# Five late modulation vectors: from TensorE products between the up products to VectorE multiplies and ScalarE row sums

## The chip, the cores and the metric

The kernel runs on one core of one Trainium2 chip, as one program in one launch. The metric is the device time of an execution in microseconds. Three runs of the kernel before gave 2391.55 (the median), 2391.75 and 2386.89 us.

## The reference, cut to what matters

Two trunk layers act on 1152 tokens of 1024 channels: 1024 sample tokens (stream 0, conditioned by `c`) and 128 prompt tokens (stream 1, conditioned by `c_ctx`). What is conditioned comes from six modulation vectors per layer and stream:

```
def modulation(cond, w_mod, b_mod):
    m = jax.nn.silu(cond) @ w_mod + b_mod          # (1024) @ (1024, 6144)
    return jnp.split(m[:, None, :], N_MOD, axis=-1)

def run_layer(x, cond, mixer, w_mod, b_mod, g_mix_pre, g_mix_post, g_ff_pre, g_ff_post, w_ff1, w_ff2):
    sh1, sc1, gt1, sh2, sc2, gt2 = modulation(cond, w_mod, b_mod)
    h = rmsnorm(x, g_mix_pre) * (1.0 + sc1) + sh1
    y, aux = mixer(h)
    x = x + gt1 * rmsnorm(y, g_mix_post)
    h = rmsnorm(x, g_ff_pre) * (1.0 + sc2) + sh2
    x = x + gt2 * rmsnorm(sq_relu_mlp(h, w_ff1, w_ff2), g_ff_post)
    return x, aux
```

`sq_relu_mlp` is relu(h @ w1) squared, times w2, with 4096 hidden channels. Everything is fp32.

## The kernel before, in words

`build` (L261) runs, one after the other: `layer0_scan` (first norm, state-space scan, Fourier mixer), `glu`, and then for each layer `mixer_out` (projection out of the mixer and the norm that precedes the MLP), `ff_up` (up product, relu, square) and `ff_down`, with `layer1_mixer` between the layers. The order of the instructions on each engine is not the program's: a scheduler sets it when the program is built, from its own timing of the instructions. Every DMA is issued by SP, in one queue.

A matmul in full precision is made of three (`mm3`, L96): each operand is split into a high part (rounded by a ScalarE copy) and a low part (a VectorE subtraction), and high times high, high times low and low times high are added up in PSUM.

`ff_up` (L951) makes the hidden channels in 16 pairs of 128-channel blocks. `pair(p)` (L963) loads two weight tiles of 512 KB (`st`, L967), forms the seven weight sums of a Strassen-like scheme, splits them (L984, L985), and runs seven products, numbered 1, 2, 6, 5, 7, 3, 4, into three PSUM tiles `puA`, `puB`, `puC`. ScalarE copies sums out (`c`, L1036), VectorE takes differences (`h`, L1040), relu and square follow (L1042 on VectorE, L1064 and L1065 on ScalarE for the last one), VectorE forms four more sums (`hsum`, L1086), and eleven DMAs store the results (L1019, L1022). The last product of a pair ends in the row `h<-puA` at L1064: from one to the next is one pair. PSUM has one buffer for each of the three tiles, and the names rotate from pair to pair.

Ten pieces of modulation (of layer 0 `gt2`, of layer 1 `gt1`, `sc2`, `sh2`, `gt2`, each in two halves of 512 outputs) are the list `K.late` (L486); `ff_up` of layer 0 calls one of them after each of its pairs 0 to 9 (L1096). A job (`mod_chunk`, L110) loads four tiles of 512 KB of `w_mod`, two into slot `E` and two into the ring `wst`, runs matmuls `pmod` (L127) with the silu of the conditioning (`csil`, 2 columns in use of 32) as the stationary operand, copies the row out (`mrow`, L131), turns it by four transposes (`pmc`, L141), and VectorE adds the four partial sums, bias and gain (L143 to L146). A gate then takes another transpose (`pmg`, L157) and a store to DRAM (L159), from where `norm_load` reads it as a broadcast.

The ring `wst` has four buffers of 128 x 1160 fp32 (L294). In `ff_up` it holds the weight tiles `st`, the sum `u7` and the modulation tiles `mst`.

Of the kernel before, what the change touches and what calls it, by code (L numbers as in the profile page):

```python
# [17 lines left out]
D = 1024  # L18
# [21 lines left out]
class Slots:  # L40


    def __init__(self, K, *names):
        self.K, self.names, self.n = K, names, 0
# [6 lines left out]
def slot(K, n, shape, dtype=F32, name=None):  # L51

    return K.slab.tile(shape, dtype, name=name or n, tag=n)
# [207 lines left out]
def build(tc, A):  # L261
# [6 lines left out]
    with ExitStack() as top:  # L268
# [37 lines left out]
        mix = glu(K, gd, yd)  # L306
        for layer in range(2):
            xq = mixer_out(K, layer, mix)
            hd, hp = ff_up(K, layer, xq, K.late if layer == 0 else ())
            acts = ff_down(K, layer, hd, hp)  # L310
            if layer == 0:
                mix = layer1_mixer(K, acts)


def layer0_scan(K):
# [3 lines left out]
    with ExitStack() as ph:  # L319
# [160 lines left out]
        with tc.tile_pool(name="s5", bufs=1, side="right", reuse_waits="tile") as s5:  # L480
            dft = fnet_jobs(K, fp, zbs, yd)
            mods = mod_jobs(K, ((0, "gt1", 2, "g_mix_post"), (0, "sc2", 4, "g_ff_pre"), (0, "sh2", 3, None),
                                (1, "sc1", 1, "g_mix_pre"), (1, "sh1", 0, None), (0, "gt2", 5, "g_ff_post"), (1, "gt1", 2, "g_mix_post"),
                                (1, "sc2", 4, "g_ff_pre"), (1, "sh2", 3, None), (1, "gt2", 5, "g_ff_post")))
            jobs = [(dft if x == "f" else mods).pop(0) for x in JSEQ]
            K.late = dft + mods  # L486
            order = [s5, s5t, s5t]

            def inputs(hb):
                W = s5_inputs_of(K, s5, hb, zd[hb // 2])  # L490
                if hb not in efs:
                    pool = order[(hb + 1) % 3]
                    if hb in spill:
                        efs[hb] = pool.tile([128, 2176], F32, name="ef", tag="ef", bufs=2 if pool is s5t else 1)
                        nc.sync.dma_start(efs[hb], spill[hb])
                    else:
                        tables(hb, pool, True)
                W.m = s5_toeplitz(K, s5, hb)
                W.et, W.f = ef_views(efs[hb])
                return W  # L500

            W = inputs(0)
            held = None
            for hb in range(HB):
                s = s5_scan(K, s5, hb, W, fin)
                now = (hb, W, s, gd[hb // 2])
                if hb + 1 < HB:
                    W = inputs(hb + 1)
                if held:
                    s5_out(K, s5, *held)  # L510
                held = now
                for job in jobs[len(jobs) * hb // HB:len(jobs) * (hb + 1) // HB]:
                    job()
            s5_out(K, s5, *held)
# [433 lines left out]
    return xq  # L948


def ff_up(K, layer, xq, jobs):  # L951

    tc, nc, A = K.tc, K.nc, K.A
    v = nc.vector
    hd = [tc.dram_tile([4, 128, 7, 512], F32, name=f"hd{layer}_{c}") for c in range(4)]
    hp = [tc.dram_tile([128, 8, 2, 2, 32], F32, name=f"hp{layer}_{c}") for c in range(4)]
    hp2, hs = Slots(K, "W3", "W4", "W5"), Slots(K, "R4", "R6")
    K.mod_row = lambda: hs.tile([128, 512], F32, "mrow")
    K.mod_tag = "t"
    K.mod_pools = [(Slots(K, "E"), "mst"), (K.wst, "st")]  # L960
    K.mod_gather = 2

    def pair(p):  # L963
        raw = []
# [128 lines left out]

    for p in range(16):
        pair(p)
        if p < len(jobs):  # L1096
            jobs[p]()
    K.mod_gather = 1
    return hd, hp


# [747 lines left out]
def host_layout(inp):  # L1849
    f = lambda n: np.asarray(inp[n])  # L1850
    a = {}
# [14 lines left out]
    for l in range(2):  # L1866
        w = f(f"l{l}_w_mod").reshape(4, 2, 128, 12, 512)
        a[f"w_mod{l}"] = np.ascontiguousarray(w.transpose(3, 2, 0, 1, 4)).reshape(12, 128, 4, 1024)
    a["x_sample"] = f("x_sample").reshape(1024, 1024)
    xp = f("x_prompt").reshape(16, 8, 1024)  # L1870
    a["xp_perm"] = np.ascontiguousarray(xp[:, ::-1].transpose(1, 0, 2)).reshape(128, 1024)
# [106 lines left out]
```

## Time and profile before

| | us |
|---|---|
| three runs, median (lowest to highest) | 2391.55 (2386.89 to 2391.75) |
| the profiled execution | 2391.31 |
| its span, first to last instruction | 2389.5 |
| PE busy (95% of the span) | 2260.6 |
| PEld (weight loads, beside PE) | 1972.7 |
| VectorE (DVE) busy (70%) | 1668.0 |
| ScalarE (ACT) busy (42%) | 994.3 |
| GpSimd (POOL) busy | 195.0 |
| mean DMA rate over the span | 151 GB/s |

Busy time is how long at least one instruction of the engine was running. An engine's instructions may overlap at their ends, so that sums of single durations come out somewhat above it. "PEclk" is the TensorE clock that was granted, as a share of full speed; "DMA" is the mean busy share of the 16 DMA engines.

### The profile page before, as it was taken

The numbers are of one execution on the slowest core, as the hardware profiler recorded it, in microseconds if no ns is written. First come the engines' busy times: TensorE is split into PE (matmuls) and PEld (weight loads), VectorE is DVE, ScalarE is ACT, GpSimd is POOL, SyncE is SP. The second block draws the span as 40 slices with busy tenths as digits, with TensorE's granted clock in tenths as the row PEclk, the third lists the DMA queues.
The fourth block names the chain that finished last, engine by engine and source line by source line (L and its number), as shares of the span: only waits on it lengthen the run. The fifth ranks groups of instructions, "written<-read, shape, count | busy, mean of one in ns | idle before, by whom it ended". The sixth has DMA issues, their size and how long they took to land.

```text
span 2389.5 us, 34799 instructions
## 1 busy us (share of the span) xinstructions
PE 2260.6 (95%) x13462; PEld 1972.7 (83%) x13462; DVE 1668.0 (70%) x2628; ACT 994.3 (42%) x1718; POOL 195.0 (8%) x213
## 2 busy tenths in 40 slices
PE   7997676999999999999999899998999999999997
PEld 4996544987788899988888699887999999888886
DVE  7888999836755555757776854857666557677778
ACT  4543333647432233443343452457333333533332
POOL 0116773200000000000000000000000000000000
PEclk9998888999999999999999899999999999999999
DMA  8375675422465563744343431122344346544433
GB/s 300 131 276 161 195 240 164 144 96 98 157 213 178 177 199 118 253 150 153 114 148 102 135 125 46 63 97 97 112 148 139 120 148 229 170 130 134 144 108 141
DMA packets 200454, 361.49 MB, mean 151 GB/s; under 512 B 50064, under 2 KB 95760, under 8 KB 198240
## 3 DMA queue, kind: packets, MB, share of 16 engines
q1 hardware_dynamic: 200288, 359.26, 45.7%
q8 instruction: 106, 1.74, 0.3%
q14 instruction: 60, 0.49, 0.1%
HBM read 256.69 MB, written 102.51 MB: 150 GB/s over the span
## 4 chain that ended last, share of the span: by engine, by line
PE 82%; DVE 11%; ACT 2%; DMA 2%; issue 1%; POOL 1%; SPq 0%; DVEq 0%; ACTq 0%
PE pz L1284 8%; PE pz L1286 8%; PE pz L1287 8%; PE puA L97 6%; PE puA L99 6%; PE puA L98 6%; PE puC L97 3%; PE puC L99 3%; PE puC L98 3%; PE po L256 3%; PE po L258 3%; PE po L257 3%; DVE tp L1780 3%; PE pmod L127 2%; PE puB L98 1%
## 5 line engine op out<-in xcount | busy, mean ns | idle before, releaser
L1284 PE MATMUL pz<-wh,hh 128*128 128x512 f32 x840 | 326.0, 389 | 1.2 <-DVE z L1298 1.2
L1287 PE MATMUL pz<-wh,hl 128*128 128x512 f32 x840 | 326.8, 389 | 0.0
L1286 PE MATMUL pz<-wl,hh 128*128 128x512 f32 x840 | 326.8, 389 | 0.0
L1272 ACT ACTIVATE hh<-hr 128x1024 fp32r<-128x1024 f32 x96 | 96.9, 1009 | 262.9 <-PE pz L1286 231.7
L1284 PEld LDWEIGHTS pz<-wh,hh 128*128 128x128 f32 x840 | 157.7, 188 | 34.5 <-issue 2.0
L1287 PEld LDWEIGHTS pz<-wh,hl 128*128 128x128 f32 x840 | 157.7, 188 | 32.7
L1286 PEld LDWEIGHTS pz<-wl,hh 128*128 128x128 f32 x840 | 157.7, 188 | 32.5
L1273 DVE TENSOR_TENSOR hl<-hr,hh 128x1024 fp32r<-128x1024 f32 x96 | 110.9, 1156 | 91.7 <-ACT hh L1272 91.7
L1298 DVE TENSOR_TENSOR z<-z,pz 128x512 f32<-128x512 f32 x192 | 122.8, 682 | 31.6 <-PE pz L1287 31.1
L984 ACT ACTIVATE wh<-c 128x512 fp32r<-128x512 f32 x96 | 60.8, 633 | 175.7 <-DVE c L993 125.8
L1040 DVE TENSOR_TENSOR h<-puA,c 128x576 f32<-128x576 f32 (+1 forms) x34 | 24.6, 722 | 147.7 <-PE puA L99 147.7
L256 PE MATMUL po<-wh,act 128*128 128x512 f32 x288 | 112.5, 394 | 1.2 <-DVE rms L906 1.2
L257 PE MATMUL po<-wl,act 128*128 128x512 f32 x288 | 113.1, 393 | 0.0
L258 PE MATMUL po<-wh,act 128*128 128x512 f32 x288 | 113.0, 393 | 0.0
L984 ACT ACTIVATE wh<-st 128x512 fp32r<-128x512 f32 x96 | 57.3, 629 | 80.5 <-DMA st<-in_w_ff_dram 27.7
L1248 DVE TENSOR_TENSOR wl<-raw,wh 128x1024 fp32r<-128x1024 f32 (+1 forms) x64 | 73.2, 1154 | 24.0 <-ACT wh L1247 24.0
L985 DVE TENSOR_TENSOR wl<-c,wh 128x512 fp32r<-128x512 f32 x96 | 66.1, 688 | 32.1 <-ACT wh L984 31.6
L92 DVE TENSOR_TENSOR wl<-st,wh 128x1024 fp32r<-128x1024 f32 (+1 forms) x42 | 52.2, 1254 | 49.9 <-ACT wh L91 49.9
L1780 DVE TENSOR_TENSOR tp<-rt,xp 128x1168 f32<-128x1168 f32 x48 | 81.1, 1728 | 7.3 <-ACT xp L1773 6.8
L985 DVE TENSOR_TENSOR wl<-st,wh 128x512 fp32r<-128x512 f32 x96 | 63.6, 686 | 27.9 <-ACT wh L984 27.8
L1036 ACT ACTIVATE c<-puA 128x576 f32<-128x576 f32 (+1 forms) x68 | 42.2, 621 | 91.9 <-PE puA L99 88.5
L127 PE MATMUL pmod<-mst,csil 128*32 128x512 f32 x384 | 77.6, 675 | 1.2 <-DMA mst<-in_w_mod_dram 1.2
(505 smaller groups left out, 6725.3 us busy)
## 6 DMA issues: line engine op xcount, KB each, us to landing
hr<-hd SPq DMA_DIRECT2D x102, 512.0 KB
mst<-in_w_mod_dram SPq DMA_DIRECT2D x96, 512.0 KB
st<-in_w_ff_dram SPq DMA_DIRECT2D x68, 512.0 KB
hd<-hsum SPq DMA_DIRECT2D x120, 256.0 KB
raw<-in_w_ff_dram SPq DMA_DIRECT2D x56, 512.0 KB
hd<-h SPq DMA_DIRECT2D x98, 256.0 KB
ef<-ef SPq DMA_DIRECT2D x16, 1088.0 KB
xr<-xs SPq DMA_DIRECT2D x32, 512.0 KB
```

Source lines behind the costliest of these rows:

```text
L97: nc.tensor.matmul(ps, sh, mh, start=start, stop=False, skip_group_check=shared)
L98: nc.tensor.matmul(ps, sh, ml, start=False, stop=False, skip_group_check=shared)
L99: nc.tensor.matmul(ps, sl, mh, start=False, stop=stop, skip_group_check=shared)
L127: nc.tensor.matmul(ps[32 * j:32 * j + 32, :], K.csil[:, kb, :], st[:, 512 * k:512 * k + 512], start=kb < 4, stop=kb >= 4, skip_group_check ...
L256: K.nc.tensor.matmul(ps, ah[kb][:, c], wh[:, s], start=kb == 0, stop=False)
L257: K.nc.tensor.matmul(ps, ah[kb][:, c], wl[:, s], start=False, stop=False)
L258: K.nc.tensor.matmul(ps, al[kb][:, c], wh[:, s], start=False, stop=kb == 7)
L985: v.tensor_tensor(wl, x, wh.bitcast(F32), op=ALU.subtract)
L1284: nc.tensor.matmul(o, hh[:, q, t], wh[:, q], start=start and s == 0 and q == 0, stop=False, skip_group_check=True)
L1286: nc.tensor.matmul(o, hh[:, q, t], wl[:, q], start=False, stop=False, skip_group_check=True)
L1287: nc.tensor.matmul(o, hl[:, q, t], wh[:, q], start=False, stop=s == 1 and q == n - 1, skip_group_check=True)
L1780: v.tensor_tensor(t[:, k], R[:, k:k + 1].to_broadcast([128, 2, 4, SC]), x, op=ALU.mult)
```

## The change

The jobs of `K.late` are gone, and with them the matmuls, the four transposes and the row copies of these five vectors. In their place a class `LateMods` makes each vector as sums along rows. The host sends the five blocks of `w_mod` turned over (`w_modt`), so that a tile of 128 x 1024 has 128 outputs on partitions and the 1024 inputs along the row. The silu of the conditioning of one stream is held in slot `E` as a tile `cs` in which all partitions have the same row; it comes from DRAM (`csd`), to which two DMAs write it from `csil`, element by element. One unit is: a DMA of 512 KB, one VectorE multiply (128 x 1024, in place, L979), and one ScalarE copy with `accum_out` (L980), which gives one column of 128 outputs for one stream. Each tile is loaded and worked on twice, once for each stream. Layer 0 has four vectors, 2 x 4 x 8 = 64 units, spread over the 15 steps after pairs 1 to 15 (four or five a step); layer 1 has one vector, 16 units, one or two a step. A vector ends with bias and gain on VectorE, and a gate with one transpose (L999) and a store.

```diff
-            hd, hp = ff_up(K, layer, xq, K.late if layer == 0 else ())
+            hd, hp = ff_up(K, layer, xq)
...
-                                (1, "sc1", 1, "g_mix_pre"), (1, "sh1", 0, None), (0, "gt2", 5, "g_ff_post"), (1, "gt1", 2, "g_mix_post"),
-                                (1, "sc2", 4, "g_ff_pre"), (1, "sh2", 3, None), (1, "gt2", 5, "g_ff_post")))
+                                (1, "sc1", 1, "g_mix_pre"), (1, "sh1", 0, None)))
...
+LATE = (((0, "gt2", 5, "g_ff_post"), (1, "gt1", 2, "g_mix_post"), (1, "sc2", 4, "g_ff_pre"), (1, "sh2", 3, None)),
+        ((1, "gt2", 5, "g_ff_post"),))
+
+class LateMods:
+    def __init__(self, K, wanted):
...
+        self.units = [(s, n, b) for s in range(2) for n in range(len(wanted)) for b in range(8)]
+        self.total, self.stream = len(self.units), None
+
+    def step(self, k, steps):
+        K, nc = self.K, self.K.nc
+        while self.units and self.total - len(self.units) < self.total * (k + 1) // steps:
+            s, n, b = self.units.pop(0)
+            layer, _, piece, _ = self.wanted[n]
+            if s != self.stream:
+                self.stream = s
+                self.c = slot(K, "E", [128, D], F32, "cs")
+                row = K.csd[s]
+                nc.sync.dma_start(self.c, bass.AP(tensor=row.tensor, offset=row.offset, ap=[[0, 128], [1, D]]))
+            st = stage_tile(K, "mst")[:, :D]
+            nc.sync.dma_start(st, K.A["w_modt"][LATE_ROWS.index((layer, piece)), b])
+            nc.vector.tensor_tensor(st, st, self.c, op=ALU.mult)
+            nc.scalar.activation(st, st, AF.Copy, accum_out=self.out[n][:, b, s:s + 1])
+            if s == 1 and b == 7:
+                self.end(n)
...
+def ff_up(K, layer, xq):
...
-    K.mod_row = lambda: hs.tile([128, 512], F32, "mrow")
-    K.mod_tag = "t"
-    K.mod_pools = [(Slots(K, "E"), "mst"), (K.wst, "st")]
-    K.mod_gather = 2
+    if layer == 0:
+        K.csd = tc.dram_tile([2, D], F32, name="csd")
+        for s in range(2):
+            nc.sync.dma_start(K.csd[s].rearrange("(k p) -> p k", p=128), K.csil[:, :, s])
+    late = LateMods(K, LATE[layer])
...
     for p in range(16):
         pair(p)
-        if p < len(jobs):
-            jobs[p]()
+        if p:
+            late.step(p - 1, 15)
```

How the built order moves at the three places that matter:

On TensorE, in a pair of layer 0 that had a job, ahead of the fourth product (`x04`). Before:

```order
L97 MATMUL puC<-x13h,wh 128x288
L98 MATMUL puC<-x13l,wh 128x288
L99 MATMUL puC<-x13h,wl 128x288
L127 MATMUL pmod<-mst,csil 32x512 x2
L97 MATMUL puA<-x04h,wh 128x288
```

and after the change:

```order
L99 MATMUL puC<-x13h,wl 128x288
L99 MATMUL puA<-x11h,wl 128x288
L97 MATMUL puA<-x11h,wh 128x288
L98 MATMUL puA<-x11l,wh 128x288
L99 MATMUL puA<-x11h,wl 128x288
L97 MATMUL puA<-x04h,wh 128x288
```

The `pmod` matmuls are gone, and the second half of the next pair's first product (`x11`) now stands in front of the fourth.

On VectorE, one pair of the changed kernel, from its second difference (`h<-puA`) on (`mst` is a modulation tile, `cs` the conditioning, `wl` a low part):

```order
L1098 TENSOR_TENSOR h<-puA,c 128x576
L1100 SCALAR_TENSOR_TENSOR h<-h 128x576
L1051 TENSOR_TENSOR c<-st 128x512
L1043 TENSOR_TENSOR wl<-c,wh 128x512
L1098 TENSOR_TENSOR h<-puC,c 128x576
L1043 TENSOR_TENSOR wl<-u,wh 128x512
L979 TENSOR_TENSOR mst<-mst,cs 128x1024
L1053 TENSOR_TENSOR c<-c,st 128x512
L1100 SCALAR_TENSOR_TENSOR h<-h 128x576
L1144 TENSOR_TENSOR hsum<-h 128x512 x2
L979 TENSOR_TENSOR mst<-mst,cs 128x1024
L1043 TENSOR_TENSOR wl<-st,wh 128x512
```

The multiplies stand among the differences, the low parts and the sums, and each of them waits for the DMA of its own tile.

On SP, at the start of the program (rows before, then rows now):

```order
L358 DMA x_136<-in_x_sample_dram 128x1024
L119 DMA mst<-in_w_mod_dram 128x1024 x16
L88 DMA st<-in_w_in_dram 128x1024 x4
```

```order
L358 DMA x_136<-in_x_sample_dram 128x1024
L119 DMA mst<-in_w_mod_dram 128x1024 x7
L1018 DMA csd<-csil 128x8x1 x2
L119 DMA mst<-in_w_mod_dram 128x1024 x9
L88 DMA st<-in_w_in_dram 128x1024 x4
```

The two stores of the conditioning, written in `ff_up`, have come to stand among the first 16 loads of the program. The order also differs in details in the first stages, whose text is the same.

## Rows read from the trace of the kernel before

**Rows 1.** The page: engines' busy time, DMA in all, the chain by engine
```profile
span 2389.5 us, 34799 instructions
PE 2260.6 (95%) x13462; PEld 1972.7 (83%) x13462; DVE 1668.0 (70%) x2628; ACT 994.3 (42%) x1718; POOL 195.0 (8%) x213
...
DMA packets 200454, 361.49 MB, mean 151 GB/s; under 512 B 50064, under 2 KB 95760, under 8 KB 198240
...
q1 hardware_dynamic: 200288, 359.26, 45.7%
...
PE 82%; DVE 11%; ACT 2%; DMA 2%; issue 1%; POOL 1%; SPq 0%; DVEq 0%; ACTq 0%
```

**Rows 2.** Busy time by stretch: ten pairs with jobs, three without, ten of layer 1
```profile
core 0: us, PE busy (x) PEld busy (x) DVE busy (x) ACT busy (x) POOL busy (x), PEclk, DMA share, GB/s
654.34:913.11 258.77, 258.77 (x1841) 230.45 (x1840) 140.49 (x234) 79.92 (x136) 0.00 (x0) 1.00 0.56 186
913.11:980.07 66.96, 66.96 (x506) 66.96 (x505) 40.47 (x64) 22.53 (x37) 0.00 (x0) 1.00 0.43 137
1779.33:2002.52 223.19, 223.19 (x1682) 223.19 (x1681) 134.92 (x211) 75.12 (x121) 0.00 (x0) 1.00 0.43 136
```

**Rows 3.** ACT in order of time: last row of a pair (start, length, idle before)
```profile
603.37 0.41 ACT L1064 ACTIVATE h<-puA 128x288 f32<-128x288 f32 x1
...
631.86 0.41 ACT L1064 ACTIVATE h<-puA 128x288 f32<-128x288 f32 x1 [1.08 <-PE puA L99]
...
654.34 0.64 ACT L1064 ACTIVATE h<-puA 128x576 f32<-128x576 f32 x1
...
913.11 0.64 ACT L1064 ACTIVATE h<-puA 128x576 f32<-128x576 f32 x1
...
1668.83 0.41 ACT L1064 ACTIVATE h<-puA 128x288 f32<-128x288 f32 x1 [0.19 <-PE puA L99]
...
1692.96 0.39 ACT L1064 ACTIVATE h<-puA 128x288 f32<-128x288 f32 x1
```

**Rows 4.** Groups on PE, 640 to 913 us: modulation matmuls and their transposes
```profile
L127 PE MATMUL pmod<-mst,csil 128*32 128x512 f32 x144 | 31.4, 604 | 0.0
L141 PE MATMUL pmc<-cst,mrow 128*128 128x128 f32 x40 | 6.0, 272 | 0.0
L157 PE MATMUL pmg<-cst,mrow 128*8 128x128 f32 x6 | 1.6, 272 | 0.0
```

**Rows 5.** Groups and one line's instructions that are like the added ones
```profile
L1237 DVE TENSOR_TENSOR u<-raw 128x1024 f32<-128x1024 f32 x14 | 17.1, 1224 | 7.3 <-DMA raw<-in_w_ff_dram 7.2
...
L189 ACT ACTIVATE junk<-z x24: 1038/1058/1062, 1326.0 to 2377.8; 128x1024 bf16<-128x1024 f32 x24
L189 ACT ACTIVATION_READ_ACCUMULATOR junk<-z x24: 186/188/199, 1327.0 to 2378.8; 128x1 f32 x24
```

**Rows 6.** Waits, 654 to 913 us: who waited for whom, total, times, longest
```profile
DVE h L1040 <- PE puA L99: 30.9, 10, 7.5
...
ACT wh L984 <- DMA st<-in_w_ff_dram: 26.0, 7, 7.1
ACT mrow L131 <- DMA hd<-hsum: 17.1, 5, 7.3
```

**Rows 7.** The start: SP's issues, a piece of the chain, busy time by stretch
```profile
4.70 29.78 SPq L119 DMA_DIRECT2D mst<-in_w_mod_dram  x16
...
40.42 1.02 PE pmod L127 x8
41.45 3.59 DMA st<-in_w_in_dram
...
0.00:20.00 20.00, 10.94 (x14) 3.13 (x14) 11.26 (x60) 7.13 (x11) 0.60 (x7) 1.00 0.89 310
20.00:32.00 12.00, 11.69 (x47) 4.30 (x46) 7.59 (x45) 2.91 (x5) 0.00 (x0) 1.00 0.46 153
32.00:45.00 13.00, 10.98 (x70) 5.41 (x70) 12.53 (x48) 6.21 (x11) 0.00 (x0) 1.00 0.89 332
```

More of the change, by code (lines that the diff above doesn't have):

```diff
@@ L482, in layer0_scan @@
             mods = mod_jobs(K, ((0, "gt1", 2, "g_mix_post"), (0, "sc2", 4, "g_ff_pre"), (0, "sh2", 3, None),
-                                (1, "sc1", 1, "g_mix_pre"), (1, "sh1", 0, None), (0, "gt2", 5, "g_ff_post"), (1, "gt1", 2, "g_mix_post"),
-                                (1, "sc2", 4, "g_ff_pre"), (1, "sh2", 3, None), (1, "gt2", 5, "g_ff_post")))
+                                (1, "sc1", 1, "g_mix_pre"), (1, "sh1", 0, None)))
             jobs = [(dft if x == "f" else mods).pop(0) for x in JSEQ]
-            K.late = dft + mods
+            assert not dft + mods
             order = [s5, s5t, s5t]
@@ L948, in mixer_out, with end @@
     return xq
-def ff_up(K, layer, xq, jobs):
+LATE = (((0, "gt2", 5, "g_ff_post"), (1, "gt1", 2, "g_mix_post"), (1, "sc2", 4, "g_ff_pre"), (1, "sh2", 3, None)),
+        ((1, "gt2", 5, "g_ff_post"),))
+class LateMods:
+    def __init__(self, K, wanted):
+        self.K, self.wanted = K, wanted
+        self.out = [K.csil[:, :, 4 + 2 * n:6 + 2 * n] if name[0] == "g" else
+                    K.const.tile([128, 8, 2], F32, name=f"mc{layer}_{piece}")
+                    for n, (layer, name, piece, _) in enumerate(wanted)]
+        self.units = [(s, n, b) for s in range(2) for n in range(len(wanted)) for b in range(8)]
[16 more added lines that the diff above has]
+                self.end(n)
+    def end(self, n):
+        K, nc, v = self.K, self.K.nc, self.K.nc.vector
+        layer, name, piece, what = self.wanted[n]
+        o = self.out[n]
+        bias = K.vec[layer]["b_mod"][:, 8 * piece:8 * piece + 8]
+        v.tensor_tensor(o, o, bias[:, :, None].to_broadcast([128, 8, 2]), op=ALU.add)
+        row = stage_tile(K, "mst") if name[0] == "g" else None
+        if what:
+            r = o if row is None else row[:, 0:16].rearrange("p (k s) -> p k s", s=2)
+            v.scalar_tensor_tensor(r, o, 1.0 if row is None else 0.0,
+                                   K.vec[layer][what][:, :, None].to_broadcast([128, 8, 2]), op0=ALU.add, op1=ALU.mult)
+        if name[0] != "g":
+            K.mod[layer][name] = o
+            return
+        pg = K.psum.tile([128, 512], F32, name="pmg", tag="t", bufs=2)
+        nc.tensor.transpose(pg[:16, :128], row[:, 0:16], K.ident)
+        nc.scalar.activation(row[:16, 128:256], pg[:16, :128], AF.Copy)
+        K.mod[layer][name] = dst = K.tc.dram_tile([2, D], F32, name=f"gate{layer}_{piece}")
+        nc.sync.dma_start(dst.rearrange("s (k n) -> k s n", n=128), row[:16, 128:256])
@@ L953, in ff_up @@
+LATE_ROWS = [(layer, piece) for part in LATE for layer, _, piece, _ in part]
+def ff_up(K, layer, xq):
     tc, nc, A = K.tc, K.nc, K.A
@@ L1095, in ff_up @@
         pair(p)
-        if p < len(jobs):
-            jobs[p]()
-    K.mod_gather = 1
+        if p:
+            late.step(p - 1, 15)
     return hd, hp
@@ L1868, in host_layout @@
         a[f"w_mod{l}"] = np.ascontiguousarray(w.transpose(3, 2, 0, 1, 4)).reshape(12, 128, 4, 1024)
+    a["w_modt"] = np.ascontiguousarray(np.stack([f(f"l{l}_w_mod")[:, 1024 * p:1024 * p + 1024].T.reshape(8, 128, 1024)
+                                                 for l, p in LATE_ROWS]))
     a["x_sample"] = f("x_sample").reshape(1024, 1024)
```

## The prediction

> **What bounds the kernel now.** I read the page first: TensorE is busy in 95% of the span and is 82% of the chain that ended last, VectorE 11% [rows 1]. So an edit is worth time only where it takes work from TensorE in a stage in which TensorE never waits, or where it makes TensorE wait. The second view is busy time by stretch. In the ten pairs of layer 0 that carry a modulation job TensorE is busy for 258.77 of 258.77 us, in the three pairs without a job for 66.96 of 66.96, in ten pairs of layer 1 for 223.19 of 223.19, always at the full clock [rows 2]. The up products are thus bound by TensorE alone. The third view is ScalarE in order of time, where the row that ends a pair gives its period: ten pairs from 654.34 to 913.11 us, 25.88 us each; without a job, and in layer 1, 22.32 us (66.96 / 3 and 223.19 / 10) [rows 2, 3]. The other engines have room there. Per pair without modulation VectorE is busy 13.49 us (40.47 / 3), ScalarE 7.51, and the DMA engines 0.43 of 22.32 = 9.6 us [rows 2].
>
> **What is removed.** The ten jobs, one after each of the pairs 0 to 9. The worth of this is read from the periods, not from the matmuls' durations: 258.77 - 10 x 22.32 = **35.6 us**. The groups say the same from the other side: pmod is 31.4 us for nine jobs in this stretch, its transposes 6.0 and the gates' 1.6, together 39.0, of which a few us are counted double where ends overlap [rows 4]. A tenth of the matmuls lies ahead of 654 us, in pair 0, where TensorE also waits for other things. The two halves of pair 0 stand 28.49 us apart in layer 0 and 24.13 in layer 1, where no job is near [rows 3]; so that job is worth between 0 and 4.4 us, and I take 1.0, since most of that difference goes with the norm's last tile, whose operands come just then. The row copies and the small VectorE sums that go too were hidden and are worth nothing.
>
> **What is added in layer 0.** 64 units on 15 pairs, 4.27 a pair. Each is a VectorE multiply; the nearest row, the same shape and type, has 1.22 us [rows 5]. 4.27 x 1.22 = 5.2, so VectorE comes to 13.49 + 5.2 = 18.7 of 22.32 us. On ScalarE a row sum is a pass of 1.06 and a read of the accumulator of 0.19 [rows 5]: 4.27 x 1.25 = 5.3, in all 12.8 of 22.32. The loads: four tiles of 512 KB a pair made 0.56 x 25.88 = 14.5 us of DMA time where 9.6 is needed without them, 1.2 us a tile [rows 2]; 4.27 of them give 9.6 + 5.2 = 14.8 of 22.32, a share of 0.66, which the 0.89 of the start shows to be possible [rows 7]. By busy time all three stay below TensorE, so the units are hidden if they do not wait in the wrong place.
>
> That is the unknown cost. A multiply stands in VectorE's queue and waits for its tile; behind it stand the differences that free a PSUM buffer which TensorE needs (the built order shows a multiply between the second difference of one pair and the next). The ring has four buffers and seven or eight tenants a pair, so that several units in a row use one buffer one after the other: load, multiply, row sum, next load. The row for one load of 512 KB that nothing else overlapped is 3.59 us [rows 7]. From below the cost is nothing, since VectorE idles 22.32 - 18.7 = 3.6 us a pair, waiting for TensorE anyway (its waits for `puA` are 30.9 us over the ten pairs, up to 7.5 [rows 6]). From above it is each load in full: 4.27 x 3.59 = 15.3 a pair, less the 3.6 idle, 11.7 x 15 = 176 us. I take **5 us**, a third of a us a pair, near the lower end: the nearest row is the stretch with jobs, where as many tiles a pair went through the same ring and queue, ScalarE waited 26.0 us for weight tiles and 17.1 for slots, and TensorE lost nothing [rows 2, 6].
>
> **Smaller parts.** Layer 1 gets 16 units, about one a pair: VectorE 13.49 + 1.3 of 22.32, hidden; 0.5 us for a wait or two, between 0 and 3.6 (one load exposed). Three gates still take one transpose of 0.27 us each [rows 4]: 0.8. The last gate is ready after pair 15 of layer 1 and is read only at the end of the down product, so it delays nothing. The stores of the conditioning, 2 x 1024 pieces of one element, now stand between the 7th and 8th of the first 16 modulation loads. These loads keep SP busy or waiting from 4.70 to 34.48 us, the DMA engines are at 0.89, then 0.46, then 0.89 again, and the chain runs through pmod and a weight load at 41.45 us [rows 7]; a delay there goes on to the end. No row has packets so small. The lower bound is 0, as they may fall in the 20 to 32 us where the engines are half idle. The upper bound is the mean packet: 45.7% of 16 engines over 2389.5 us for 200288 packets is 87 ns each [rows 1], so 2048 of them take 178 us on one engine and 11 us on sixteen. I take **3 us**: small packets should be below the mean, and half of that time is idle.
>
> The Trainium skill, DMA: Bandwidth & Descriptors, in its rules for kernel authors, says that a transfer whose last dimension is not contiguous becomes one descriptor for each element, and advises against it. Of this the trace of before shows nothing; taken at the mean packet's price it would put the sum at 2372 instead of 2364, which is inside one of the cases below.
>
> **The sum**, against the profiled execution's own time of 2391.31 us (its span is 2389.5; the median of the runs is 2391.55, so that no correction is needed): 2391.3 - 35.6 - 1.0 + 5 + 0.5 + 0.8 + 3 = **2364.0 us**, or 1.1% faster.
>
> **The rivals.**
> *Nothing is given back.* All waits fall into VectorE's 3.6 us a pair and the stores into the idle stretch: 2391.3 - 36.6 + 0.8 = 2355.5, and 2352 if pair 0 gains its whole 4.4. For it speaks that TensorE was at 100% with as many DMAs; against it that a pair is now 3.56 us shorter and VectorE goes from 14.0 of 25.88 to 18.7 of 22.32.
> *A third to a half is given back.* VectorE waits 1 us a pair beyond its idle time (+15 in place of +5), or the stores cost their upper bound (+11 in place of +3): 2372 to 2385, say 2377. For it speaks the deep chain of one buffer; against it that the built order runs parts of the next pair's first product ahead of the fourth, which gives a late difference some slack.
> *No change.* The period is set by VectorE at 22.32 + 36 / 15 = 24.7 us, which needs (24.7 - 18.7) / 4.27 = 1.4 us of waiting per multiply. That is within 0.2% (4.8 us) of before, about what a measurement of this kernel can tell from no change. It needs a coincidence.
> *Slower: VectorE's queue stands behind the loads.* Each multiply waits more than 1.4 us for its tile, in a place where the next difference is due, and the pair is paced by VectorE. At 2 us each the period is 18.7 + 8.5 = 27.2, so 15 x 4.9 = 73 us more than at TensorE's pace: 2391.3 - 36.6 + 73 + 4 = 2432. For it: the scheduler's places were set by its own timing of a load, and loads take 3.59 us alone and longer beside stores. Against it: between two multiplies stand on the whole four or five other VectorE instructions, some 3 us of work, and ScalarE and SP are free enough to start the next load at once.
> That the change does not do what it says is excluded by the built order: the matmuls are gone from TensorE.
>
> **How the numbers follow.** Forecast (2358 to 2371) 0.43; nothing given back 0.17; a third to a half 0.20; no change 0.05; slower 0.15. The first three are faster by more than 0.2%: 0.80. The range goes from 2350, just below the best case, to 2392, where the no-change case lies; it leaves out the slower case and a little more, some 0.17.
>
> **What the profile of after would show.** Right: the last row of a pair at L1123 every 22.3 to 22.7 us from pair 2 on in layer 0, TensorE busy all the time there, VectorE near 18 us and ScalarE near 12 a pair, no pmod later than the scan stage, layer 1's pairs at 22.32. The first weight load and the first pz products up to 3 us later than before. Wrong in the slower way: pairs of 25 us or more, VectorE's multiply waiting for DMA at the head of the waits, TensorE waiting for `h` at L1098 or for `wl` at L1043. Wrong at the start: the loads behind the two stores landing some 10 us late with everything after them. If layer 0's pairs are at 22.4 and the time is still above 2375, the loss is in the first 400 us, where the order moved in details.

## The result and the profile after

The change made the kernel slower: 2406.49 us (2404.23 to 2407.54) against 2391.51 us, ratio 1.0071, 95% interval 1.0058 to 1.0084. The forecast was 2364.0 with a range of 2350 to 2392: wrong side, outside the range. The profiled execution took 2404.23 us.

The page of the kernel after, against [rows 1]: TensorE has 22 us less to do, yet the span is 13 us longer, and DMA has risen from 2% to 9% of the chain that ended last.
```profile
span 2402.4 us, 34675 instructions
PE 2238.9 (93%) x13259; PEld 1975.3 (82%) x13259; DVE 1754.6 (73%) x2689; ACT 1070.9 (45%) x1867; POOL 194.6 (8%) x213
...
DMA packets 208870, 384.55 MB, mean 160 GB/s; under 512 B 52848, under 2 KB 98544, under 8 KB 206656
...
PE 70%; DVE 14%; DMA 9%; ACT 3%; issue 2%; POOL 1%; SPq 0%; DVEq 0%; ACTq 0%
```

ScalarE in order of time, the last row of a pair, against [rows 3] (L1122 is L1064 of before):
```profile
605.75 0.41 ACT L1122 ACTIVATE h<-puA 128x288 f32<-128x288 f32 x1 [0.18 <-PE puA L99]
...
639.88 0.39 ACT L1122 ACTIVATE h<-puA 128x288 f32<-128x288 f32 x1
...
663.43 0.63 ACT L1122 ACTIVATE h<-puA 128x576 f32<-128x576 f32 x1
...
1004.69 0.63 ACT L1122 ACTIVATE h<-puA 128x576 f32<-128x576 f32 x1
...
1676.60 0.41 ACT L1122 ACTIVATE h<-puA 128x288 f32<-128x288 f32 x1 [0.24 <-PE puA L99]
...
1705.59 0.39 ACT L1122 ACTIVATE h<-puA 128x288 f32<-128x288 f32 x1
```
The end of pair 15 in the kernel before, which [rows 3] does not have:
```profile
1002.65 0.65 ACT L1064 ACTIVATE h<-puA 128x576 f32<-128x576 f32 x1 [6.84 <-PE puA L99]
```
Pair 0 of layer 0 takes 34.1 us instead of 28.5. Pairs 1 to 15 take 364.8; the same rows of before stand at 631.86 and 1002.65, 370.8 us, so dropping the jobs won 6.0 of some 36. From there to layer 1's pair 0 it takes 671.9 us instead of 666.2, and that pair 29.0 instead of 24.1. Layer 1's other pairs, with a unit each, are unchanged (332.0 against 332.1).

Busy time by stretch, against [rows 2]: pairs 1 to 15 of layer 0, and three pieces around one stall.
```profile
639.88:1004.69 364.81, 341.04 (x2474) 333.60 (x2472) 271.63 (x377) 171.74 (x300) 0.00 (x0) 0.99 0.67 219
...
818.00:825.50 7.50, 4.85 (x37) 4.61 (x36) 3.78 (x5) 2.65 (x5) 0.00 (x0) 1.00 0.95 325
825.50:829.00 3.50, 3.50 (x17) 3.50 (x16) 1.89 (x3) 2.40 (x5) 0.00 (x0) 0.51 0.62 223
829.00:836.00 7.00, 7.00 (x55) 7.00 (x54) 5.78 (x9) 2.33 (x5) 0.00 (x0) 1.00 0.15 43
```
TensorE is idle for 364.81 - 341.04 = 23.8 us of a stretch in which it was hardly idle before, while VectorE is busy for only 74% of it and ScalarE for 47%: a queue that waits in the wrong place, not a full engine. The last three rows show what this stall cost besides itself: TensorE stands for 2.65 us, and in the next 3.5 us the granted clock is 0.51, the 1.2 GHz level, with 17 matmuls recorded in 3.5 us where the following 7.0 us have 55. These fifteen pairs hold three such stretches of 3.4 us (from 699.2, 825.5 and 897.2 us); after the other stalls the clock stays at full speed.

The waits of 634 to 1010 us, then SP's of 640 to 1005, against [rows 6]:
```profile
ACT mst L980 <- DVE mst L979: 106.8, 43, 6.1
DVE mst L979 <- DMA mst<-in_w_modt_dram: 54.6, 33, 3.7
...
ACT wh L1042 <- DMA st<-in_w_ff_dram: 18.4, 8, 3.9
...
PE puA L97 <- ACT wh L1042: 7.0, 5, 2.3
```
```profile
SPq L978 <- ACT mst L980: 105.9, 29, 6.5
...
SPq L1025 <- ACT mst L980: 12.4, 10, 4.4
```
The circle can be read off: SP waits for a row sum to free one of the ring's four buffers, then issues the load; VectorE waits for the load; ScalarE's row sum waits for VectorE. Each wait stands in an in-order queue, and behind it are the things that TensorE needs.

One stall in order of time, VectorE, ScalarE and TensorE of the kernel after:
```profile
818.07 0.75 DVE L1100 SCALAR_TENSOR_TENSOR h<-h 128x576 f32<-128x576 f32 x1
822.18 1.23 DVE L979 TENSOR_TENSOR mst<-mst,cs 128x1024 f32<-128x1024 f32 x1 [3.36 <-DMA cs<-csd]
...
818.18 0.63 ACT L1042 ACTIVATE wh<-c 128x512 fp32r<-128x512 f32 x1 [2.47 <-DVE c L1059]
823.44 1.06 ACT L980 ACTIVATE mst<-mst 128x1024 f32<-128x1024 f32 x1 [4.62 <-DVE mst L979]
...
824.49 0.63 ACT L1094 ACTIVATE c<-puA 128x576 f32<-128x576 f32 x1
...
822.23 0.29 PE L99 MATMUL puC<-x15h,wl 128*128 128x288 f32 x1
825.18 0.40 PE L97 MATMUL puA<-x07h,wh 128*128 128x288 f32 x1 [2.65 <-ACT c L1094]
```
VectorE waits 3.36 us for the conditioning row of the second stream (elsewhere it is the tile of a unit, as in the waits above). ScalarE has issued the row sum of that multiply and stands for 4.62 us. The copy of `puA` at 824.49, which frees the PSUM buffer for the next product, stands behind the sum, and TensorE waits 2.65 us for it.

### The profile page after: what moved, and what is told of

Read it like the earlier page. It is cut to its first block, busy times and chain, and to the rows that moved or that the text cites. A ratio compares the mean times of both kernels' runs of the same rounds, so it can differ in the third digit from the quotient of the medians.

```text
span 2402.4 us, 34675 instructions
## 1 busy us (share of the span) xinstructions
PE 2238.9 (93%) x13259; PEld 1975.3 (82%) x13259; DVE 1754.6 (73%) x2689; ACT 1070.9 (45%) x1867; POOL 194.6 (8%) x213
## 4 chain that ended last, share of the span: by engine, by line
PE 70%; DVE 14%; DMA 9%; ACT 3%; issue 2%; POOL 1%; SPq 0%; DVEq 0%; ACTq 0%
PE pz L1343 8%; PE pz L1341 8%; PE pz L1344 8%; DMA mst<-in_w_modt_dram 4%; PE puA L99 3%; PE puA L97 3%; PE puA L98 3%; DVE tp L1837 3%; PE po L256 3%; PE po L258 3%; PE po L257 3%; DMA st<-in_w_ff_dram 2%; PE puC L97 2%; PE puC L98 2%; PE puC L99 2%
## 5 line engine op out<-in xcount | busy, mean ns | idle before, releaser
L979 DVE TENSOR_TENSOR mst<-mst,cs 128x1024 f32<-128x1024 f32 x80 | 97.9, 1223 | 70.1 <-DMA mst<-in_w_modt_dram 65.0
L980 ACT ACTIVATE mst<-mst 128x1024 f32<-128x1024 f32 x80 | 84.6, 1057 | 122.0 <-DVE mst L979 121.1
L1305 DVE TENSOR_TENSOR wl<-u,wh 128x1024 fp32r<-128x1024 f32 x64 | 73.6, 1152 | 4.9 <-ACT wh L1304 4.9
L1304 ACT ACTIVATE wh<-raw 128x1024 fp32r<-128x1024 f32 (+1 forms) x64 | 62.9, 995 | 32.1 <-PE ppr L1316 24.2
```

The source lines that it names most:

```text
L1305: v.tensor_tensor(wl, w, wh.bitcast(F32), op=ALU.subtract)
```

## Experiments

The theories were: **A**, the queues of VectorE (and ScalarE) stand behind loads; **B**, the units' engine work itself; **C**, the added traffic; **S**, SP's queue and the ring: weight tiles come late behind loads that wait for a buffer; **D**, the removal is worth little. Each run is given with its median and its ratio to the kernel before, run on the same chip; that kernel's own median went from 2388.8 to 2391.5 us from chip to chip, so a difference of 2 or 3 us between two runs of this list says nothing. "Pairs" is the time from the end of pair 0 to the end of pair 15 in layer 0, read as above from the profiled execution (before 370.8, after 364.8).

### What the removal is worth, and what each part of a unit costs

**No units.**
```
-            st = stage_tile(K, "mst")[:, :D]
-            nc.sync.dma_start(st, K.A["w_modt"][...])
-            nc.vector.tensor_tensor(st, st, self.c, op=ALU.mult)
-            nc.scalar.activation(st, st, AF.Copy, accum_out=...)
+        (zeros in the five vectors)
```


> Left out: the loads, multiplies and row sums of the late vectors in both layers, so that the five vectors hold only bias and gain; the stores of the conditioning and the gates' transposes stay. Theory A (VectorE's multiplies stand in its queue and wait for tiles whose loads start late, because several units in a row use one buffer of the ring): all of the given-back time is gone, 2352 to 2362 us, pairs of 22.3 to 22.8 us, pair 0 of both layers as long as before or shorter. Theory B (the multiplies' and sums' own busy time, no waiting): the same. Theory C (the added 40 MB of loads delay the weight tiles): the same. Theory D (taking the TensorE jobs away is worth little, since the loss comes from the changed order elsewhere, the start and the transitions): 2380 us or more.

2360.5 us, 0.9878 (0.9863 to 0.9893); pairs 332.3, pair 0 26.3, layer 1's pair 0 27.4. D is out. The units cost 2406.5 - 2360.5 = 46.0 us. Its pairs (busy time by stretch):
```profile
635.90:968.20 332.30, 330.90 (x2482) 329.87 (x2481) 205.04 (x315) 112.43 (x181) 0.11 (x1) 1.00 0.48 153
```
So of the 32.5 us that the units cost in the pairs, 23.8 - 1.4 = 22.4 is TensorE idle, and 341.04 - 330.90 = 10.1 is TensorE busy for longer with the same products. The three stretches at half the clock, 10.2 us in all, account for some 5 of these 10.1; the rest stays open.

**Engine work without loads.**
```
-            nc.sync.dma_start(st, K.A["w_modt"][...])
-            nc.vector.tensor_tensor(st, st, self.c, op=ALU.mult)
+            nc.vector.tensor_tensor(st, self.c, self.c, op=ALU.mult)
```


> Left out: the loads of the weight tiles of the late vectors; each multiply takes the conditioning row twice instead (a wrong vector), into the same ring buffer, and the row sums stay. Theory A: without a load there is nothing to wait for, 2355 to 2368 us, VectorE's waits for DMA in these pairs gone, PE gaps in layer 0's pairs below 8 us in sum (24 with the loads). Theory B: all engine work is there, so 2395 to 2406 us. Theory C: the traffic is gone, 2355 to 2368, so this run does not tell it from A.

2372.2 us, 0.9920 (0.9903 to 0.9937); pairs 338.4, pair 0 32.1. The work costs 11.7 us: some 6 in the pairs and 6 in pair 0. B is not the main cause, nor is it nothing.

**Loads alone.**
```
-            nc.vector.tensor_tensor(st, st, self.c, op=ALU.mult)
-            nc.scalar.activation(st, st, AF.Copy, accum_out=...)
+        (zeros in the five vectors)
```


> Left out: the multiplies and row sums; all 80 loads stay, into the same ring. Theory A: VectorE and ScalarE have no queue entry that waits for these tiles, and a buffer is free again once its load has landed: 2355 to 2370 us. Theory B: the same, 2355 to 2362. Theory C: the traffic and the ring's tenants are all there, so most of the loss stays, 2390 to 2406 us, with ScalarE's and VectorE's waits for st tiles as long as in the changed kernel.

2382.6 us, 0.9974 (0.9964 to 0.9985); pairs 355.8. Loads that nobody reads cost 22.1 us, which A did not expect. Its waits (634 to 990 us), engines, then SP:
```profile
DVE u L1056 <- DMA st<-in_w_ff_dram: 47.6, 11, 9.4
...
ACT wh L1042 <- DMA st<-in_w_ff_dram: 40.8, 10, 9.0
```
```profile
SPq L980 <- DMA mst<-in_w_modt_dram: 113.8, 41, 4.7
SPq L1025 <- DMA mst<-in_w_modt_dram: 28.7, 10, 3.2
```
The weight tiles `st` come late, and SP waits 142 us at ring buffers that a unit's load holds. This is S, or still C. The order on TensorE, ScalarE and VectorE is, but for some twenty places, that of the run without units, so a changed order is an unlikely rival here.

**Loads and multiplies, no row sums.**
```
-            nc.scalar.activation(st, st, AF.Copy, accum_out=...)
+        (zeros in the five vectors)
```


> Left out: the row sums on ScalarE; loads and multiplies stay. In the changed kernel ScalarE waits 106.8 us in layer 0's pairs at the row sums for the multiply, with the casts of the weights behind them in its queue, and VectorE 54.6 us at the multiplies for the tiles. Theory A1 (VectorE's waits are what holds TensorE): 2395 to 2406 us. Theory A2 (ScalarE's waits are): 2380 to 2388, near the 2382.6 of the loads alone. Theory B2 (ScalarE's 80 us of busy time): 2395 to 2400.

2403.6 us, 1.0053 (1.0038 to 1.0068); pairs 368.5. The multiplies add 20.9 us to the loads, nearly twice what multiplies and sums cost together without loads; the sums add only 2.9. VectorE's waits suffice (A1); with them there, ScalarE's add next to nothing.

### Traffic, SP's queue or the ring

**Small loads in the same places.**
```
-            nc.sync.dma_start(st, K.A["w_modt"][..., b])
+            nc.sync.dma_start(st[:, :8], K.A["w_modt"][..., b, :, :8])
```
(without multiplies and sums)


> Left out: multiplies and row sums, and of each load all but 8 of 1024 columns; the 80 loads stand in SP's queue and in the ring as in the run with loads alone, with 1/128 of their traffic. Theory C: the cost of 22 us goes, 2358 to 2364 us. Theory S: SP still waits for each small load to land before it issues the next one into the same buffer, though a small one lands sooner (estimate 2 us against 3.6 to 4.4), so about half or less of the cost stays: 2363 to 2374 us.

2361.1 us, 0.9880 (0.9865 to 0.9895); pairs 332.3. The whole cost is gone, which alone would speak for C. But SP's wait at these loads fell too, from 113.8 to 45.9 us, so the run does not tell C from S; S had expected some cost to stay.

**Full loads, outside ring and SP's queue**, twice.
```
-            st = stage_tile(K, "mst")[:, :D]
-            nc.sync.dma_start(st, ...)
+            st = slot(K, "E", [128, D], F32, "mst")
+            nc.gpsimd.dma_start(st, ...)
```


> Left out: multiplies and row sums as in the run with loads alone; the 80 loads go to one buffer outside the ring (that of the conditioning rows, which are not loaded) and are issued from GpSimd's queue, so that neither the ring nor SP's queue sees them. The loads alone cost 22 us (2382.6 against 2360.5). Theory C (the traffic of the added loads slows the weight tiles): that cost stays, 2375 to 2385 us. Theory S (SP's queue stands in order: each load of a unit waits there for its ring buffer, 41 waits with 114 us in layer 0's pairs, and the loads of the weight tiles stand behind it): the cost goes, 2358 to 2364 us, pairs of 22.3.

> The run with the loads alone from GpSimd's queue into a buffer outside the ring, again, with the zeros of the five vectors (that run wrote them from GpSimd, behind its loads, and one pair of it stood 40 us for that: DVE waited 45.1 us for POOL csil) written by VectorE instead. Left out: multiplies and row sums. All its other pairs were 22.3 us. Theory C (traffic): 2375 to 2385 us. Theory S (the order of SP's queue and the ring): 2357 to 2364 us.

2402.6 us (1.0053) and 2402.2 us (1.0053), but not for the traffic: in the first, all of the 42 us lie in one pair of 64.3 us, where VectorE waits 45.1 us for zeros that GpSimd writes behind its loads. In the second it is again one pair, of 64.2, for another reason; its waits, of the engines (925 to 970 us) and of SP (634 to 1000):
```profile
ACT wh L1037 <- DMA st<-in_w_ff_dram: 47.4, 1, 47.4
```
```profile
SPq L705 <- DMA mst<-in_w_modt_dram: 57.7, 3, 49.6
```
L705 is a load that the next stage wants in the same buffer E; SP waits for E, and a weight tile behind it in SP's queue is 47.4 us late. Ahead of it, with the loads running, TensorE does not stand once in 220 us, at a higher DMA share than the changed kernel's 0.67:
```profile
660.00:880.00 220.00, 220.00 (x1658) 219.96 (x1657) 134.94 (x213) 73.72 (x120) 22.59 (x44) 1.00 0.73 230
```
C is out, and both accidents show at full size how one waiting entry of an in-order queue holds up what stands behind it.

**Loads alone in the ring, from GpSimd's queue.**
```
-            nc.sync.dma_start(st, K.A["w_modt"][...])
+            nc.gpsimd.dma_start(st, K.A["w_modt"][...])
```
(without multiplies and sums)


> Left out: multiplies and row sums, as in the run of 2382.6 us with the loads alone; the loads go into the ring as there but are issued from GpSimd's queue (the zeros of the five vectors are written by VectorE). Theory S1 (the weight tiles' loads stand in SP's queue behind loads that wait for a buffer): 2357 to 2364 us. Theory S2 (it is the buffers of the ring themselves that the weight tiles lack): 2374 to 2384 us.

2369.7 us, 0.9918 (0.9900 to 0.9937); pairs 343.2. Between S1 and S2: of the 22.1 us, 12.9 go with SP's queue, 9.2 stay with the ring (SP still waits 48.4 us at L1025 for a buffer that a unit holds). The order on SP and VectorE changed with this edit too, so the split is rough. Its pairs by busy time:
```profile
637.30:980.50 343.20, 334.08 (x2484) 330.63 (x2483) 205.98 (x315) 111.22 (x181) 31.76 (x60) 1.00 0.73 237
```
TensorE stands for 9.1 us here, at the full clock throughout.

**The changed kernel with these loads from GpSimd's queue** (the same edit, nothing left out).


> Nothing left out: only the 80 loads of the units are issued from GpSimd's queue in place of SP's; ring, multiplies and row sums stay. Theory S: SP's queue holds only the weight tiles and stores again, so the 22 us of the loads go for the most part and what is left is the engine work of 12 us and some multiplies that wait: 2372 to 2388 us. Theory A (VectorE's multiplies that wait for tiles are the main cost): 2395 to 2406. Theory C: 2395 to 2406 as well.

2403.0 us, 1.0054 (1.0037 to 1.0071); pairs 362.1. A miss for S: with the multiplies there, freeing SP's queue alone gives nothing that counts; VectorE still waits 46.4 us for tiles. The two causes do not add: take one away and the other still holds TensorE.

### Other engines, other places

**The multiplies on GpSimd.**
```
-            nc.vector.tensor_tensor(st, st, self.c, op=ALU.mult)
+            nc.gpsimd.tensor_tensor(st, st, self.c, op=ALU.mult)
```


> Nothing left out: the 80 multiplies run on GpSimd, which has nothing else to do there, in place of VectorE; loads and row sums stay. Theory A: a late tile now holds up only GpSimd's queue, so TensorE's gaps go: 2358 to 2375 us. What a multiply costs on GpSimd is not in any trace so far; if it takes 3 us, 64 are 192 of some 340 us, which fits. Theory B with VectorE's busy time as the cause: 2358 to 2375 too; with ScalarE's: 2400. Theory C: 2400 us. If GpSimd's work slows VectorE's own instructions: VectorE's 720 ns differences come out longer in the rows and the time lies above 2380.

2420.3 us, 1.0128 (1.0113 to 1.0143); pairs 378.8. A miss. The multiply on GpSimd (its instructions from 640 to 1005 us, min/median/max in ns) and who waits for it:
```profile
L979 POOL TENSOR_TENSOR mst<-mst,cs x59: 2338/2593/5901, 638.3 to 1003.0; 128x1024 f32<-128x1024 f32 x59
```
```profile
ACT mst L980 <- POOL mst L979: 125.7, 44, 7.0
```
The chain of load, multiply, sum got 1.4 us longer, and the wait moved to ScalarE's queue; VectorE's differences kept their 0.75 us.

**A later start.**
```
-        if p:
-            late.step(p - 1, 15)
+        if p > 2:                       # layer 0
+            late.step(p - 3, 13)
```


> Nothing left out: in layer 0 the 64 units stand behind the pairs 3 to 15 in place of 1 to 15 (4.9 a pair). Pair 0 of layer 0 took 34.1 us with units against 26.3 without them; all theories expect that to come back, some 6 to 8 us. Theory S and A: the pairs behind get denser and give 1 to 4 of it back, in all 2399 to 2404 us. A rival: the cost per unit rises with their density, and the time is 2407 us or more.

2400.3 us, 1.0046 (1.0031 to 1.0061); pair 0 27.5 instead of 34.1, pairs 366.6. As expected: the scheduler had drawn units into pair 0, where TensorE waited 4.6 us for `h` and 4.5 for `x15h`.

**Fixed places**: one unit at each of five places of a pair, tied behind a VectorE instruction there, loaded two places earlier. Both changes of buffers of the next part are in this run too.
```
+        with K.tc.issue_after(after.ins):
+            nc.vector.tensor_tensor(st, st, self.c, op=ALU.mult)
...
+        st = slot(K, "W5", [128, D], F32, "mst") if self.turn % 2 else stage_tile(K, "mst")[:, :D]
```


> Nothing left out. Each unit is loaded at one of five places of a pair and multiplied two places later, right behind a VectorE instruction of that place, so that its tile has long landed; every other unit has a buffer of its own (one of the three of h), the other one takes the place in the ring of the sum u, which moves to the buffer of the squares. No unit stands in pair 0. Theory A (the queues of VectorE and ScalarE stand behind loads): what is left is engine work, some 6 us in the pairs (338.4 against 332.3 in the run without loads), so 2364 to 2375 us, with VectorE's waits for these tiles near nothing. Theory B: 2395 or more. Theory S: SP no longer waits for the ring as long, 2370 to 2385.

2433.7 us, 1.0179 (1.0164 to 1.0194); pairs 405.9, the slowest of all. The waits (634 to 1040 us):
```profile
ACT mst L997 <- DVE mst L996: 98.0, 49, 4.9
DVE wl L1060 <- ACT wh L1059: 55.6, 25, 6.3
ACT wh L1059 <- DMA st<-in_w_ff_dram: 33.3, 14, 5.5
...
DVE mst L996 <- DMA mst<-in_w_modt_dram: 8.6, 6, 2.4
```
VectorE's waits for tiles are nearly gone (8.6 us), as meant, and it is slower by 27 us, and by 51.5 us than the next run, which has the same buffers and leaves the places to the scheduler. Only the multiply was tied: ScalarE has the sum early in its queue and waits 98.0 us for it, casts wait behind, and weight tiles are late. So "VectorE waits for loads" is too small a theory: the waits point to whichever in-order queue stands in front of a tile's chain. That is read from the waits; no run takes the sums out of this one.

### Buffers

**Two changes of buffers**: every other unit in one of the three buffers of `h`, and the sum `u` out of the ring into the buffer of the squares.
```
+            st = slot(K, "W5", ...) if self.turn % 2 else stage_tile(K, "mst")[:, :D]
-    hp2 = Slots(K, "W3", "W4", "W5")
+    hp2 = Slots(K, "W3", "W4")
-        u7 = stage_tile(K, "u")[:, :512]
+        u7 = K.small.tile([128, 512], F32, name="junk", tag="junk", bufs=1)
```


> Nothing left out. Only the buffers of the run with fixed places: every other unit in one of the three buffers of h, the sum u out of the ring; the units' places are left to the scheduler as in the changed kernel. If the one-buffer chain is the cause: 2375 to 2390 us. If the places are (loads land later than the scheduler's order supposes): 2396 to 2406, and pair 0 of layer 0 stays near 34 us. If two buffers for h are too few: longer than the changed kernel, with VectorE's h waiting for the stores hd.

2382.2 us, 0.9962 (0.9949 to 0.9975): **faster than both kernels**, 24 us below the changed one, with all its work; pairs 344.0. Waits (634 to 1040 us) and busy time of the pairs:
```profile
ACT mst L981 <- DVE mst L980: 69.0, 44, 5.6
DVE mst L980 <- DMA mst<-in_w_modt_dram: 33.7, 26, 3.6
```
```profile
640.90:984.90 344.00, 335.35 (x2482) 332.06 (x2483) 271.40 (x378) 172.96 (x295) 0.00 (x0) 1.00 0.74 235
```
VectorE does the same work (271.40 us) and TensorE's idle time falls from 23.8 to 8.7.

**Each change alone** (`u` out of the ring; the buffer of `h`).


> Nothing left out: of the two changes of buffers only the first, the sum u out of the ring; units as in the changed kernel, all in the ring. If the number of tenants of the ring is what matters: 2385 to 2396 us. If it is that the units follow each other in one buffer: 2398 to 2406.

> Nothing left out: only the second change of buffers, every other unit in one of the three buffers of h; u stays in the ring. If the chain of one buffer matters: 2382 to 2394 us. If the number of the ring's tenants: 2396 to 2406. If two buffers for h are too few on their own: above 2400, with VectorE's h waiting for hd.

2414.4 us, 1.0099 (1.0084 to 1.0114), and 2412.1 us, 1.0087 (1.0072 to 1.0102): neither alone gives anything back (the interval of the second overlaps that of the changed kernel). With `u` alone VectorE's wait for tiles is as long as before (53.9 us) and SP waits 40.1 us with weight tiles for units' sums; with the buffer of `h` alone the wait for tiles is 67.5 us, and pair 0 takes 36.5 us. TensorE's idle time in the pairs is 23.0 and 24.8 us, against 23.8 in the changed kernel. With `u` alone, layer 1's pairs, which have a unit each, take 18.5 us longer than in the changed kernel, at the full clock:
```profile
1700.93:2051.46 350.53, 339.39 (x2497) 334.74 (x2496) 223.64 (x331) 123.82 (x211) 0.00 (x0) 1.00 0.52 172
```
VectorE waits for tiles for only 2.4 us there (1760 to 2010 us), so this loss is not the one of layer 0. Neither "number of tenants" nor "one buffer" explains the pair of them. The scheduler also draws another order for each edit, and these runs do not separate buffers from order.

**Both changes and a later start.**
```
+        if p > 2:
+            late.step(p - 3, 13)
```


> Nothing left out: the buffers of the run that took 2382.2 us, and no unit behind the pairs 0 to 2 of either layer (4.9 a pair after them in layer 0, 1.2 in layer 1). In that run pair 0 of layer 0 took 32.5 us against 26.3 without units, pair 0 of layer 1 30.9 against 27.4. Theory P (units that the scheduler draws into pair 0 meet engines that are already late there): 5 to 9 us come back, 2372 to 2378 us. Rival (density costs as much as it gives): 2379 to 2386.

2387.3 us, 0.9991 (0.9981 to 1.0000). A miss: pair 0 still takes 31.3 us (layer 1's 30.5) and the denser pairs 354.7. The edit did not do what it said. With a buffer free for it, the scheduler drew the first multiplies into pair 0 all the same, where VectorE in order of time has
```profile
608.42 1.23 DVE L980 TENSOR_TENSOR mst<-mst,cs 128x1024 f32<-128x1024 f32 x1 [2.45 <-DMA cs<-csd]
```
In the later start without the buffers the first one stands at 666.18 us.

**The same without the one-element stores.**
```
-            nc.sync.dma_start(K.csd[s].rearrange("(k p) -> p k", p=128), K.csil[:, :, s])
+                nc.scalar.activation(self.c, self.c, AF.Silu)   # rows loaded raw
```


> Nothing left out: as the run before it, and the conditioning rows are loaded raw from the inputs and put through Silu on ScalarE, so that the 2 x 1024 one-element stores of the start are gone. The first end of pair 0 stands at 605.7 to 610.2 us in all runs with these stores and at 603.4 in the kernel before. Theory Q (the stores delay the start): it comes back to 603 to 605 and the time is 2 to 6 us below the run before it. Rival (the order of the early loads is changed by more than the stores): no difference beyond 2 us.

2390.1 us, 1.0006 (0.9994 to 1.0018): no gain. The first end of pair 0 stands at 605.0 us against 605.5. Near the start, though, the stores do show. SP in order of time, with the stores (the run above) and then without, and busy time from 20 to 32 us likewise:
```profile
12.57 4.98 SPq L1019 DMA_DIRECT2D csd<-csil  x2
18.02 19.39 SPq L119 DMA_DIRECT2D mst<-in_w_mod_dram  x9
```
```profile
4.70 25.03 SPq L119 DMA_DIRECT2D mst<-in_w_mod_dram  x16
```
```profile
20.00:32.00 12.00, 10.50 (x44) 3.63 (x45) 7.64 (x46) 2.69 (x4) 0.00 (x0) 1.00 0.62 86
20.00:32.00 12.00, 9.24 (x63) 3.86 (x60) 10.08 (x55) 4.82 (x8) 0.00 (x0) 1.00 0.81 268
```
With the stores the DMA engines move 86 GB/s there instead of 268, SP has issued the 16 loads at 37.4 us instead of 29.7, and the first weight product (`pz`) starts at 46.34 instead of 41.50. Of these 4.8 us only 0.5 are left at pair 0. The order of the early instructions changes with the edit, so that not all of the 4.8 need be the stores'. The Trainium skill (DMA: Bandwidth & Descriptors, Rules for kernel authors) says that a transfer whose last dimension is not contiguous becomes one descriptor for each element, and advises against it. The trace agrees at the start, with 86 against 268 GB/s; no run here shows a price in the whole time.

**Both buffer changes, loads from GpSimd's queue.**


> Nothing left out: the kernel of 2382.2 us (both changes of buffers), and the 80 loads of the units issued from GpSimd's queue. In that kernel SP still waits 43 and 37 us for the units' row sums, ahead of loads of units and of weight tiles. Theory S (SP's order is the greater part of what is left there): 2368 to 2378 us. Theory A (what is left is multiplies that wait, 33.7 us): 2379 to 2388.

2382.4 us, 0.9973 (0.9962 to 0.9983), level with the run without it. The Trainium skill, Perfetto Trace Analysis, DMA Optimizations, suggests one queue for inputs and another for outputs. That split was not tried: here a second queue took the side loads alone, which was worth 12.9 us where only the loads stood in the way, and nothing where their readers waited too.

## Why the prediction was wrong

*What bounds the kernel* was right: without units every pair but pair 0 runs at TensorE's pace. The busy times were right too: a pair of the changed kernel has 18.1 us of VectorE (271.63 / 15; 18.7 forecast), 11.4 of ScalarE (12.8) and a DMA share of 0.67 (0.66).

*What is removed* was right in sum, by luck in part. Without added work the terms give 2391.3 - 35.6 - 1.0 + 0.8 + 3 = 2358.5; measured 2360.5. By place: pairs 38.5 saved, pair 0 2.2 (taken as 1.0), but the start 6.2 us later and layer 1's pair 0 3.3 longer. The 3 for the stores had its mechanism right: the chain of the changed kernel runs through two waits for modulation loads near the start, which the chain of before does not have (us from the start, length):
```profile
17.67 13.34 DMA mst<-in_w_mod_dram
...
35.50 7.61 DMA mst<-in_w_mod_dram
```
Its first weight product starts 1.5 us later (45.85 against 44.39). That the first end of pair 0 is then 2.4 us later, near the 3, is luck: it moves by 2 to 7 us from kernel to kernel, and comes 1.7 us later than before even without the stores. What happens to it on the way stays open.

*What is added in layer 0* is **the step that failed: the 5 us for multiplies that wait**, out of bounds of 0 to 176. With the 0.5 for layer 1 it stood for 5.5 of the units' 46.0 us. By place, with and without units in the profiled executions (44.1 us in all): the pairs 32.5, pair 0 7.8, from pair 15 to layer 1's pair 0 6.1, that pair 1.6, less 3.8 at the start. The 6.1 lie mostly in the first 26 us behind pair 15, here with units and then without:
```profile
1004.69:1030.69 26.00, 23.70 (x92) 19.08 (x93) 17.56 (x15) 11.40 (x16) 0.00 (x0) 0.87 0.81 284
```
```profile
968.22:994.22 26.00, 26.00 (x116) 21.49 (x115) 18.51 (x17) 15.51 (x20) 0.00 (x0) 1.00 0.65 205
```
Three things were wrong in the step.

First, the row that drew it to the low end. "As many tiles a pair went through the same ring and queue, and TensorE lost nothing": the number of loads was the same, but not who read them. A job's tile was read by TensorE, so a late tile held back no queue but TensorE's own, in a stage where the job was TensorE's work. A unit's tile holds VectorE, then ScalarE, then SP, and comes free after three steps instead of one: from 654 to 913 us SP waited 18.0 us at these loads (12 times) before; from 663 to 913 it waits 76.1 (21 times) now.

Second, the slack. VectorE's 3.6 idle us a pair were subtracted as if any wait could use them. The multiplies wait 60.4 / 64 = 0.94 us each (605 to 1005 us), well below the 1.4 from which the slower rival was to decide, and VectorE is busy for 74%: it never sets the pace. TensorE stops where one wait meets one due copy, cast or difference, as in the stall above. (The 3.59 us a load "that nothing else overlapped", behind the upper bound, was read where the DMA engines were busy for 0.89 [rows 7]: it is not the time of a load alone.) The slower rival named the right queue, with the wrong condition and price: it needs no paced engine.

Third, what was counted at nothing. Loads that nobody reads cost 22.1 us, roughly 12.9 through SP's order and 9.2 through the ring; engine work without loads costs 11.7, half of it in pair 0; and a TensorE that is busy for longer is 10.1 of the 32.5 us in the pairs, about half of it put down to the stretches at 1.2 GHz. By the Trainium skill, Perfetto Trace Analysis, Optimization Strategy, repeated gaps on the engine that should be full can mean that no buffer is free for the next tile. The run with both changes of buffers agrees, with TensorE's idle time at 8.7 instead of 23.8 us; the two with one change each do not (23.0 and 24.8), so that no run here settles it.

*Layer 1*: pairs right (332.0); its pair 0 was not counted: 4.9 us, of which 3.3 come without any unit.

Shown is that the cost hangs on the loads and on what waits for them: without loads 34 of the 46 us go, and with loads that nothing waits for, outside ring and SP's queue, TensorE is busy for 220.00 of 220.00 us. How it divides between the queues and the ring is argued from waits. Open: why the two changes of buffers help together and not apart, what the scheduler's other order did in each run with multiplies, and what moves the start and layer 1's pair 0. A kernel with multiply and sum both held back until the tile has landed was not tried.

## What to carry to other kernels

Busy shares say whether work fits an engine, not whether it fits its queue: for each added instruction that waits for a load, ask what stands behind it in that in-order queue, SP's included, and who frees its buffer. A stretch with as many loads is no evidence if other engines read them. When work moves off the bounding engine into a shared ring, run once without the work and once with its loads alone before shifting it between engines; here two changes of buffers together gave back 24 us, and another engine cost 14.

## What the runs showed of the hardware

A 128x1024 multiply of fp32 tiles in SBUF takes a median of 1225 ns on VectorE (the changed kernel) and of 2593 on GpSimd. Where the traffic ran beside the products, outside the ring and SP's queue, TensorE was busy for 220.00 of 220.00 us at a DMA share of 0.73. A stall of 2.65 us was followed by 3.5 us at a granted clock of 0.51, so that it cost more than its own length; 9.1 us of stalls in the pairs of the run with the loads alone from GpSimd's queue were followed by none. While two stores of 1024 single elements each were under way, the DMA engines moved 86 GB/s from 20 to 32 us, against 268 in the run without them, whose early order differs too.
